# Statistics of one head group by way of DRAM, and four more chunks of products ahead of the first scores, in a two-layer encoder on one core

## The chip, the core and the metric

The kernel runs on one core of a Trainium2 chip. A core has a matrix engine (TensorE, in the profile PE for its matmuls and PEld for its weight loads), a vector engine (DVE), an activation engine (ACT), a general engine (GpSimd, POOL) and a queue for transfers (SyncE, SP); ACT and POOL can start transfers too. The metric is the device time of one launch in microseconds (us), as the median of the runs. The profile is that of one more execution, taken by the hardware profiler; its times are counted from the first instruction of its span.

## The reference

The input is x, 512 tokens of 1024 features, in float32. There are two layers; each is an attention and a SwiGLU feed-forward of width 2816, both with an RMS norm ahead and a residual behind, and a last RMS norm ends it. Layer 0 has 16 query heads on 4 key heads, a window of 128 tokens to either side, a penalty that grows with distance, and a learned sink logit for each head. Layer 1 is where most of the change lies:

```python
for gi, (win, dil) in enumerate(((128, 1), (512, 4), (2048, 16))):
    q, k, v = (to_residue(qkv[:, :, gi, n], dil) for n in range(3))
    o, lse = banded_attention(q, k, v, slopes, dil, win // (2 * dil), 64)
    outs.append(from_residue(o, b, dil)); lses.append(from_residue(lse, b, dil))
wts = softmax(stack(lses), axis=0)
o = einsum('gbsh,gbshd->bshd', wts, stack(outs))
x = x + o.reshape(b, s, 1024) @ w_out
```

For each of 16 head slots there are three groups of query, key and value. Group 0 attends to neighbours within 64 tokens; groups 1 and 2 to tokens of the same residue class modulo 4 and 16. The three outputs are added with weights from their softmax denominators. So whoever finishes a head slot needs, for each token, the maximum and the sum of the exponentials of group 0.

## The kernel before, in words

All activations lie transposed, features on the 128 partitions and the 512 tokens along the free dimension. Every product of float32 is made of three matmuls on operands that are split into a high and a low part (`mm3`, line 116). A weight unit is 128 output features by 1024 inputs: SP loads it into one of three buffers `wraw`, ACT writes the high part `wh` (line 92), DVE the low part `wl` (line 93). TensorE then runs it in 8 steps of 6 matmuls of 256 columns; such a step is a *chunk* here. Units of values (`values`, line 192, tile `psv`) have 16 chunks of the same 6 matmuls.

TensorE's instructions run in the order in which the program is written. The other engines' order is set by a scheduler when the program is built; each engine then runs its own list, and waits where a result of another engine is not there yet. The PSUM tiles go round in tags: three banks `mm`, two `sc`, two `tp`, one `ov`.

Since a chunk depends on nothing near it, chunks are used as filling. A generator `fill` hands them out, and `spread` and `weave` (lines 156 to 171) place a number of them between the steps of the attention: scores, turning of the probabilities (transposes on TensorE), weighing of the values.

**Layer 0, start.** The first key and query units end before the sum of squares is known. `norm_sums` (line 258) and `norm_rows` (line 267) then make 1/rms as columns and as rows; at the end of `norm_rows` the waiting keys and queries are scaled and split on DVE and ACT (lines 123 to 138, 310, 320). After it the program places 6 chunks of the unit of values, then the first scores, with chunks between them:

```python
spread([2, norm_sums, 4, norm_rows], early)
counts = [8, 9, 7, 6, 6, 6, 4, 4, 4, 4, 3, 2, 2, 2, 3, 3]
spread([6, s0, 1, s1, 1, s2, 1, s3, 2], fill)
```

`early` is that unit of values: 2 and 4 of its 16 chunks lie ahead of the rows, 10 behind them, then `fill` goes on with query units. Its four blocks of tokens are gathered in the banks `ov`, `sc`, `tp`, `mm`, 4 chunks each, and copied out by ACT (line 205, tile `v`). s0 to s3 are the scores of the first two attention units. Each has two score tiles, which take the two `sc` banks; DVE adds the distance table and takes the maximum (line 349), ACT takes the exponential with its sum (line 356), DVE the reciprocal (358), POOL multiplies (360), and TensorE turns the result (367). `counts` says how many chunks go into each of the 16 attention units that follow.

**Layer 1.** For each of 8 pairs of heads p, `attention_a(p)` does group 0 (four blocks t of 128 queries; `scores_a`, `turn_a`, `weigh_a`) and `attention_b(p)` groups 1 and 2 (`scores_b`, `turn_b`, `merge_rows`, `weigh_b`), each woven with 32 chunks (48 in the first). `scores_a` leaves in the tile `sta`, for each query on its partition, the negative maxima and the sums of two heads (lines 670 and 672). Group 0 has its queries in another order than groups 1 and 2, which work by residue class, so the statistics must change their order. `merge_turn` (line 783) turns `sta` on TensorE into 4 rows (tile `stt`), which DVE copies in the new order into `strow` (line 791); `merge_back` (line 798) turns these back with 4 small transposes (tile `stc`), and DVE copies them into `sa` (line 804). `scores_b` reads `sa` for the first time in its line 734, on DVE. So that the transpose sees 128 columns, `sta` is a padded tile that POOL sets to zero at the layer's start (line 590).

**End.** `final` (line 454) writes the last 256 tokens: transposes, a scaling by 1/rms on ACT and DVE, four transfers out.

## Time and profile before

| | us |
|---|---|
| median of 3 runs (range) | 1468.41 (1467.15 to 1469.77) |
| the profiled execution | 1470.46 |
| its span | 1468.3 |
| PE busy in the span | 1452.2 |
| DVE, ACT, POOL busy | 731.5, 613.4, 107.4 |
| mean granted TensorE clock | 0.995 of full |

The stages in the span: layer 0's attention with its projections until about 185, its feed-forward until 551, layer 1's attention until about 1098, its feed-forward until 1462, then the transfers out.

How to read it: a row of the timeline has start, duration, engine, line, operation, output<-inputs, count of merged instructions, and in brackets how long the engine had been idle and who released it. A row of the windows has, for a stretch of the span, its length, the busy time of TensorE (with the number of instructions), the granted clock, the share of the transfer engines and GB/s. Matmuls overlap in the pipeline, so that the time of one row is longer than the distance to the next; what a matmul costs is read from the distance of the starts.

### The profile page before, as it was taken

To read this page: it belongs to the slowest core of one execution; us is meant where nothing else is said; L and a number is where in the kernel's file an instruction comes from. 1 tells how busy PE (TensorE), PEld (TensorE's weight loads), DVE (VectorE), ACT (ScalarE), POOL (GpSimd) and SP (SyncE) were. 2 spreads that over 40 slices of the span, in tenths; PEclk is the share of its full clock that TensorE was granted. 3 is DMA by queue.
4 is the path that set the end of the run, shared out by engine and by line. 5 is a ranking of instruction groups with operands and counts; after the bars stand their busy time and mean duration, and the time that the engine had idled before them with its cause. 6 is when DMAs were issued, how large, how long until landed. Compare 5 with 4: busy or idle time off the path is not lost.

```text
span 1468.3 us, 29636 instructions
## 1 busy us (share of the span) xinstructions
PE 1452.2 (99%) x12834; PEld 1426.0 (97%) x12834; DVE 731.5 (50%) x1393; ACT 613.4 (42%) x1130; POOL 107.4 (7%) x150
## 2 busy tenths in 40 slices
PE   8999999999999999999999999999999999999998
PEld 8888999999999999999999999999999999999998
DVE  6677544444443335346556556556464444443223
ACT  5676442332223325435536536536343233222222
POOL 4234200000000100000000000000030000000111
PEclk9999999999999999999999999999999999999999
DMA  6110223223223232322122222221133223322231
GB/s 202 58 44 30 79 94 102 88 100 101 99 84 107 90 100 85 102 73 87 59 87 73 73 87 73 73 83 63 58 103 99 99 89 101 101 96 96 94 98 65
DMA packets 38354, 128.29 MB, mean 87 GB/s; under 512 B 4560, under 2 KB 6096, under 8 KB 38224
## 3 DMA queue, kind: packets, MB, share of 16 engines
q1 hardware_dynamic: 37792, 125.86, 25.8%
q8 instruction: 100, 1.64, 0.5%
q10 hardware_dynamic: 432, 0.54, 0.1%
q14 instruction: 30, 0.25, 0.1%
HBM read 124.29 MB, written 2.10 MB: 86 GB/s over the span
## 4 chain that ended last, share of the span: by engine, by line
PE 94%; ACT 2%; DVE 2%; issue 1%; DMA 0%; POOL 0%; SPq 0%; DVEq 0%; ACTq 0%; POOLq 0%
PE mm L121 51%; PE sc L121 16%; PE psv L121 10%; PE tp L121 8%; PE sc L718 1%; PE sc L659 1%; PE sc L143 1%; PE ov L381 1%; PE ov L773 1%; PE tp L367 1%; PE tp L681 1%; PE ov L700 1%; ACT pr L356 0%; PE tp L760 0%; DVE wl L93 0%
## 5 line engine op out<-in xcount | busy, mean ns | idle before, releaser
L92 ACT ACTIVATE wh<-wraw 128x1024 fp32r<-128x1024 f32 (+3 forms) x242 | 247.2, 1024 | 599.5 <-PE mm L121 254.4
L93 DVE TENSOR_TENSOR wl<-wraw,wh 128x1024 fp32r<-128x1024 f32 (+3 forms) x242 | 289.3, 1196 | 201.5 <-ACT wh L92 197.6
L121 PE MATMUL mm<-xh,wh 128*128 128x256 f32 x1632 | 331.5, 285 | 1.4 <-ACT wh L92 1.4
L121 PE MATMUL mm<-xh,wl 128*128 128x256 f32 x1632 | 321.4, 279 | 0.8 <-DVE wl L93 0.7
L121 PE MATMUL mm<-xl,wh 128*128 128x256 f32 x1632 | 321.4, 279 | 0.0
L121 PEld LDWEIGHTS mm<-xh,wh 128*128 128x128 f32 x1632 | 248.8, 189 | 7.2 <-issue 4.8
L121 PEld LDWEIGHTS mm<-xh,wl 128*128 128x128 f32 x1632 | 248.1, 189 | 1.3 <-DVE wl L93 1.2
L121 PEld LDWEIGHTS mm<-xl,wh 128*128 128x128 f32 x1632 | 248.8, 189 | 0.0
L235 POOL TENSOR_TENSOR ssum<-ssum,tmp 128x512 f32<-128x512 f32 x34 | 53.8, 1584 | 988.8 <-ACT tmp L231 974.1
L121 PE MATMUL psv<-wh,xh 128*128 128x256 f32 x288 | 83.2, 289 | 0.0
L121 PE MATMUL psv<-wl,xh 128*128 128x256 f32 x288 | 80.8, 281 | 0.0
L121 PE MATMUL psv<-wh,xl 128*128 128x256 f32 x288 | 80.8, 280 | 0.0
L121 PE MATMUL mm<-ah,wl 128*128 128x256 f32 x374 | 74.8, 276 | 0.0
L121 PE MATMUL mm<-ah,wh 128*128 128x256 f32 x374 | 74.8, 277 | 0.0
L121 PE MATMUL mm<-al,wh 128*128 128x256 f32 x374 | 74.6, 276 | 0.0
L121 PE MATMUL tp<-xh,wh 128*128 128x256 f32 x352 | 68.9, 277 | 0.0
L121 PE MATMUL sc<-xh,wh 128*128 128x256 f32 x352 | 68.8, 277 | 0.0
L121 PE MATMUL tp<-xh,wl 128*128 128x256 f32 x352 | 68.7, 276 | 0.0
L121 PE MATMUL tp<-xl,wh 128*128 128x256 f32 x352 | 68.6, 276 | 0.0
L121 PE MATMUL sc<-xh,wl 128*128 128x256 f32 x352 | 68.5, 276 | 0.0
L121 PE MATMUL sc<-xl,wh 128*128 128x256 f32 x352 | 68.5, 276 | 0.0
L121 PE MATMUL sc<-ah,wl 128*128 128x256 f32 x330 | 66.1, 276 | 0.0
(181 smaller groups left out, 2732.2 us busy)
## 6 DMA issues: line engine op xcount, KB each, us to landing
wraw<-wunits SPq DMA_DIRECT2D x191, 512.0 KB, 3.3
wraw<-wv SPq DMA_DIRECT2D x25, 512.0 KB, 3.4
wraw<-wunits SPq DMA_DIRECT2D x16, 384.0 KB, 2.9
x<-xT SPq DMA_DIRECT2D x8, 256.0 KB, 4.8
wraw<-wunits SPq DMA_DIRECT2D x4, 256.0 KB, 4.8
outT<-x SPq DMA_DIRECT2D x2, 384.0 KB, 2.8
wraw<-wunits SPq DMA_DIRECT2D x4, 128.0 KB, 4.8
tab<-tabs SPq DMA_DIRECT2D x1, 512.0 KB, 4.9
```

What stands on the lines that cost most here:

```text
L92: nc.scalar.activation(out_h, src, AF.Copy)
L93: nc.vector.tensor_tensor(out_l, src, out_h.bitcast(F32), op=OP.subtract)
L121: nc.tensor.matmul(out[:, cols], a, b[:, cols], start=first and k == 0 and c == 0, stop=last and k == 2, skip_group_check=True)
L143: nc.tensor.matmul(outs[a], qp[a][:, qc], k[a][:, kc], start=first and k is kp, stop=k is low, skip_group_check=True)
L235: nc.gpsimd.tensor_tensor(norm["sum"], norm["sum"], sq, op=OP.add)
L367: nc.tensor.transpose(tp[:, 256 * hf + 128 * i:256 * hf + 128 * i + 128], st["pr"][:, 2 * i + hf, 128 * kb:128 * kb + 128], ident)
L381: nc.tensor.matmul(ov[64 * hf:64 * hf + 64, :256], v0[:, k0 // 128 + kb, vs], st["pt", kb][:, 256 * hf:256 * hf + 256], start=(kb == 0), s ...
L659: nc.tensor.matmul(out, qk["qs", p][a][:, 128 * t:128 * t + 128], kp[k], start=t == ts[0] and k == 0, stop=k == 1, skip_group_check=True)
L681: nc.tensor.transpose(tp[:, (nb * a + kb) * 128:(nb * a + kb) * 128 + 128], st["pr", p, ts][:, a, o + 128 * kb:o + 128 * kb + 128], ident)
L700: nc.tensor.matmul(ov[rows, 128 * t - 64:128 * t + 64], v[:, t - 1 + kb, vs], pt[:, 256 * a + 128 * kb:256 * a + 128 * kb + 128], start=Fa ...
L718: nc.tensor.matmul(ps[a][:, o:o + 128], qk["q", p, 1 + g][rows, cols], qk["k", p, 1 + g][rows, cols], start=(o == 0), stop=True, skip_grou ...
L773: nc.tensor.matmul(ov[rows, 128 * c:128 * c + 128], vals[p // 2, 1 + g][:, c, hv + 64 * a:hv + 64 * a + 64], pts[g][:, 256 * a + 128 * (c ...
```

## The change

Three edits:

1. Layer 0: 10 chunks, not 6, lie between `norm_rows` and s0; the first four attention units get one chunk less each, so that the total is the same.
2. Layer 1: `merge_turn` and `merge_back` go. `merge` writes `sta` (now 16 numbers on each partition, without padding and without the zeroing) to a DRAM tile with two transfers and reads it back in the order of groups 1 and 2 with four, all started by POOL. In `attention_a` it stands ahead of the first turning; the turnings of t = 0 and 1 move one place back, and the number of places stays 13.
3. `final`: the tiles for the output are halves of two `wraw` buffers, and `last` takes a buffer of `tmp`.

```diff
-        counts = [8, 9, 7, 6, 6, 6, 4, 4, 4, 4, 3, 2, 2, 2, 3, 3]
+        counts = [7, 8, 6, 5, 6, 6, 4, 4, 4, 4, 3, 2, 2, 2, 3, 3]
...
-        spread([6, s0, 1, s1, 1, s2, 1, s3, 2], fill)
+        spread([10, s0, 1, s1, 1, s2, 1, s3, 2], fill)
...
-        last = spool.tile([128, 256], F32, name="last", bufs=1)
+        last = spool.tile([128, S], F32, name="tmp")[:, :256]
...
+        outs = [wpool.tile([128, D], F32, name="wraw") for _ in range(2)]
...
-                out = spool.tile([128, 512], F32, name="tmp" if k else "out")
+                out = outs[b][:, 512 * k:512 * k + 512]
...
-        stats = [pool.tile([128, 4, 32], F32, name=f"sta{k}", bufs=1) for k in range(2)]
-        for t in stats:
-            nc.gpsimd.memset(t, 0.0)
+        dram = ctx.enter_context(tc.tile_pool(name="dram", bufs=2, space=bass.MemoryType.DRAM))
...
-                st["sta", p] = stats[p % 2]
+                st["sta", p] = pool.tile([128, 4, 4], F32, name="sta")
...
-        def merge_turn(p):
-            ps = bank("tp", "stt")
-            nc.tensor.transpose(ps[:, :128], st["sta", p].rearrange("p t e -> p (t e)"), ident)
...
-        def merge_back(p):
...
+        def merge(p):
+            sta = st["sta", p]
+            by_query = dram.tile([S + 64, 4], F32, name="stats")
+            nc.gpsimd.dma_start(by_query[:S].rearrange("(t q) e -> q t e", t=4), sta)
+            nc.gpsimd.dma_start(by_query[S:], sta[:64, 0, :])
 
             sa = st["sa", p] = pool.tile([128, 4, 4], F32, name="sa")
-            nc.vector.tensor_copy(sa.rearrange("p c e -> p (c e)"), ps[:, :16])
+            by_class = by_query[64:].rearrange("(m c i) e -> i m c e", c=4, i=4)
+            for i in range(4):
+                nc.gpsimd.dma_start(sa[32 * i:32 * i + 32], by_class[i])
...
-                    lambda: turn((0, 1), 0), lambda: turn((0, 1), 1), lambda: merge_turn(p),
-                    lambda: turn((2, 3), 2), 0, lambda: turn((2, 3), 3), lambda: merge_back(p), 0, weigh]
+                    lambda: merge(p), lambda: turn((0, 1), 0), lambda: turn((0, 1), 1),
+                    lambda: turn((2, 3), 2), 0, lambda: turn((2, 3), 3), 0, 0, weigh]
```

How it moves instructions. First ACT's list in layer 0, from the last queries of the first scores (`qt`) to the exponentials of s0 to s3 (257 columns for s0 and s1, 385 for s2 and s3); `v` are the copies of the blocks of values, `wh` the high part of a weight unit:

```order
 L130 ACTIVATE qt_432<-tmp 64x512
 L130 ACTIVATE qt_433<-tmp 64x512
-L205 ACTIVATE v_99<-psv,rstd 128x256 x2
+L205 ACTIVATE v_99<-psv,rstd 128x256 x3
+L92 ACTIVATE wh<-wraw 128x1024
 L356 ACT_TABLE_LOAD
 L356 ACTIVATE pr,mst<-pr,mst 128x257 x4
+L92 ACTIVATE wh<-wraw 128x1024
 L356 ACTIVATE pr,mst<-pr,mst 128x385 x4
```

A third copy of values and two weight splits, which stood behind the exponentials, now stand ahead of them or among them.

Then DVE's list in layer 1, pair 0, from the turnings of group 0 to the stretch ahead of the first maxima of groups 1 and 2. Before:

```order
L93 TENSOR_TENSOR wl<-wraw,wh 128x1024
L791 COPY strow<-stt 4x4x16 x2
L791 COPY strow<-stt 4x8x16 x3
L615 TENSOR_TENSOR k_7191<-mm,rb 128x512
L93 TENSOR_TENSOR wl<-wraw,wh 128x1024
L633 COPY pt_7245<-tp 128x512
L804 COPY sa<-stc 128x16
L93 TENSOR_TENSOR wl<-wraw,wh 128x1024 x2
```

With the change (line 631 is the former 633, 613 the former 615):

```order
L93 TENSOR_TENSOR wl<-wraw,wh 128x1024
L631 COPY pt_7145<-tp 128x512
L613 TENSOR_TENSOR k_7190<-mm,rb 128x512
L93 TENSOR_TENSOR wl<-wraw,wh 128x1024
L631 COPY pt_7244<-tp 128x512
L93 TENSOR_TENSOR wl<-wraw,wh 128x1024 x2
```

The five copies to `strow` and the copy to `sa` are gone; a turning's copy (`pt`) moved behind a weight split.

Last, POOL's list with the change, from the end of layer 0 to the end of pair 0's statistics (788 and 787 write to DRAM, 793 reads back):

```order
L235 TENSOR_TENSOR ssum<-ssum,tmp 128x512 x14
L848 COPY acca<-ssum 128x512
L788 DMA stats<-sta 64x4
L787 DMA stats<-sta 128x4x4
L793 DMA sa<-stats 32x4x4 x4
```

The three rows of transfers stand there eight times, once for each pair; POOL has nothing else between them.

## The prediction

> **What bounds the kernel now.** I read the page's first part, then the chain of waits, then the timeline of the two places that the change touches.

> ```profile
> PE 1452.2 (99%) x12834; PEld 1426.0 (97%) x12834; DVE 731.5 (50%) x1393; ACT 613.4 (42%) x1130; POOL 107.4 (7%) x150
> ```

> TensorE is busy 99% of the span; nothing else comes near. So time falls only where TensorE gets less work, waits less, or runs at a higher clock. Its timeline around the first scores of layer 0, then ACT's, DVE's and POOL's:

> ```profile
> 36.15 0.28 PE L121 MATMUL psv<-wh,xl 128*128 128x256 f32 x1
> 38.68 0.39 PE L143 MATMUL sc<-kt,qt 128*128 128x256 f32 x1 [2.25 <-DVE qt L131]
> 38.90 0.28 PE L143 MATMUL sc<-kl,qt 128*128 128x256 f32 x1
> 40.41 0.58 PE L143 MATMUL sc<-kt,qt 128*128 128x256 f32 x1 [1.23 <-ACT v L205]
> ...
> 37.28 2.58 ACT L130 ACTIVATE qt<-tmp 64x512 fp32r<-64x512 f32 x4
> 39.89 0.84 ACT L205 ACTIVATE v<-psv,rstd 128x256 f32<-128x256 f32 x2
> 43.54 1.28 ACT L356 ACT_TABLE_LOAD   x1 [2.81 <-DVE mst L353]
> 44.83 0.51 ACT L356 ACTIVATE pr<-pr,mst 128x257 f32<-128x257 f32 x1
> ...
> 37.94 2.84 DVE L131 TENSOR_TENSOR qt<-tmp,qt 64x512 fp32r<-64x512 f32 x4 [1.43 <-ACT qt L130]
> 40.81 0.42 DVE L349 CUSTOM_DVE_ANT_0 pr<-sc,tab 128x256 f32<-128x256 f32 x1
> ...
> 48.07 4.10 POOL L360 TENSOR_SCALAR pr<-pr,mst 128x256 f32<-128x256 f32 x8 [24.88 <-DVE mst L358]
> ```

> TensorE runs out of chunks at 36.4 and waits twice: 2.25 us for the split queries, 1.23 us for a bank that ACT has to copy out. What follows is dearer than the waits themselves. The windows of TensorE, cut where the clock changes:

> ```profile
> 5.55:8.96 3.41, 1.96 (x14) 1.00 1.03 374
> 36.27:39.68 3.41, 0.66 (x4) 1.00 0.00 0
> 39.68:43.09 3.41, 2.68 (x12) 0.50 0.01 2
> 43.09:46.50 3.41, 3.41 (x16) 0.50 0.01 2
> 1056.84:1060.25 3.41, 2.42 (x19) 1.00 0.00 0
> ```

> The clock changes on a grid of 3.41 us. After a stretch with 0.66 us of work it is half for 6.8 us; a stretch with 1.96 us of work was followed by half clock too (8.96 to 12.37), one with 2.42 us was not. The price of a chunk stands in the chain of waits:

> ```profile
> 41.21 1.28 PE psv L121 x6
> ...
> 50.30 1.42 PE mm L121 x12
> ```

> 6 matmuls take 1.28 us at half clock, 0.71 us (0.118 each) at full.

> **The change part by part.** *Edit 1, ten chunks.* Ten chunks from the end of the rows' transposes at 31.95 last until 39.05; before, six lasted until 36.4. DVE splits a query tile in 0.71 us (2.84/4), so the first is ready at 38.65: the wait of 2.25 us is gone. The bank is not ready sooner, since ACT's rows ahead of its copy are unchanged: the second score still starts at 40.41, and a wait of about 1.0 us stays (39.45 to 40.41).

> From there I walk on with these rows: a read of scores on DVE 0.42 us, or 0.56 for 384 columns; table load 1.28; exponential 0.5; POOL 0.51 (4.10/8).

> ```profile
> 45.30 0.56 DVE L349 CUSTOM_DVE_ANT_0 pr<-sc,tab 128x384 f32<-128x384 f32 x1 [1.29 <-PE sc L143]
> ...
> L92 ACT ACTIVATE wh<-wraw 128x1024 fp32r<-128x1024 f32 (+3 forms) x242 | 247.2, 1024 | 599.5 <-PE mm L121 254.4
> L93 DVE TENSOR_TENSOR wl<-wraw,wh 128x1024 fp32r<-128x1024 f32 (+3 forms) x242 | 289.3, 1196 | 201.5 <-ACT wh L92 197.6
> ...
> 50.06 0.48 PE L121 MATMUL mm<-xh,wh 128*128 128x256 f32 x2
> ...
> 57.60 0.60 PE L367 MATMUL tp<-ident,pr 128*128 128x128 f32 x4
> ```

> TensorE: s0 ends 40.65, a chunk to 41.35, s1 to 41.97 (0.14 us for a bank), a chunk to 42.67, s2 to 43.35, a chunk to 44.05. s3 needs the banks of s2. DVE has read s1 by 42.72, splits the weights that now stand there (to 43.95), reads s2's first tile by 44.66; its next instruction waits for s0's exponentials. ACT makes them after three copies (41.15), a weight split (42.2) and the table load (43.5), so by 44.6; DVE reads s2's second tile by 45.42. s3 thus waits 0.67 and 0.42 us and ends at 45.82; two chunks to 47.2. The first turning needs POOL's four heads, which I place at 47.27, and ends at about 47.7. Before, the first chunk after that turning starts at 50.06. So TensorE is 2.4 us earlier there, and four chunks further (2.8 us): **5.2 us**. It loses 2.2 us in new or remaining waits, nowhere more than about 1.0 us in any stretch of 3.41, which leaves about 2.4 us of work, as much as in the stretch at 1056.84 that kept full clock. Bounds: 7.4 us if those waits vanish, 1.8 us if half clock comes back for two stretches (3.4 us).

> [...]

> The first four attention units give the four chunks back, one each (0.7 us). What covers that is the lead of the softmax: POOL finishes the second unit's four heads at 52.17 (48.07 and 4.10) and TensorE turns them at 57.60, 5.4 us later. If that cover were short, each unit would cost up to 0.7 us, 2.8 in all. I take 0.

> *Edit 2, the statistics.* TensorE loses, for each pair, one transpose and four small ones:

> ```profile
> 630.69 0.39 PE L121 MATMUL mm<-xh,wl 128*128 128x256 f32 x2
> 630.92 0.27 PE L786 MATMUL stt<-ident,sta 128*128 128x128 f32 x1
> 630.95 0.48 PE L121 MATMUL mm<-xh,wh 128*128 128x256 f32 x2
> 631.26 0.40 PE L121 MATMUL mm<-xl,wh 128*128 128x256 f32 x2
> ...
> 641.59 0.28 PE L121 MATMUL psv<-wh,xl 128*128 128x256 f32 x1
> 641.79 0.41 PE L801 MATMUL stc<-ident,strow 4*128 4x4 f32 x4
> 642.13 0.39 PE L121 MATMUL psv<-wh,xh 128*128 128x256 f32 x1
> 642.35 0.28 PE L121 MATMUL psv<-wl,xh 128*128 128x256 f32 x1
> ...
> 572.00:1056.00 484.00, 484.00 (x4488) 473.95 (x4487) 261.91 (x665) 241.64 (x549) 0.00 (x0) 1.00 0.23 77
> ```

> From 630.69 to 631.26 pass 0.57 us in which four matmuls of 0.118 run: the transpose costs 0.10. From 641.59 to 642.35 pass 0.76 us for two matmuls: the four small ones cost 0.52, dear for their size. So 0.62 us a pair, **5.0 us** for eight. In this stage TensorE is busy 484.00 of 484.00 us, so this comes off the end. DVE's six copies lie beside TensorE's work and give nothing.

> What is added lies on POOL and the transfer queues. POOL is free there (0.00 us busy). The new wait: DVE's line 734 reads `sa`, and everything behind it on DVE waits with it. From the last sum of group 0 to that line pass, in the last pair, 22.4 us:

> ```profile
> 1027.85 0.19 ACT L672 ACTIVATION_READ_ACCUMULATOR pr<-pr,sta 128x1 f32 x1
> ...
> 1050.43 0.16 DVE L734 SCALAR_TENSOR_TENSOR mb<-mb,sa 128x4 f32<-128x4 f32 x1
> ...
> 827.99 1.70 ACT L750 ACTIVATE pr<-pr,mb 128x256 f32<-128x256 f32 x4
> ...
> 833.74 0.60 PE L760 MATMUL tp<-ident,pr 128*128 128x128 f32 x4
> ...
> g_sb<-gains ACTq DMA_DIRECT2D x1, 20.0 KB, 3.0
> qs_sb<-qsc SPq DMA_DIRECT2D x1, 8.0 KB, 4.8
> L235 POOL TENSOR_TENSOR ssum<-ssum,tmp 128x512 f32<-128x512 f32 x34 | 53.8, 1584 | 988.8 <-ACT tmp L231 974.1
> ```

> No row shows a transfer started by POOL. Nearest: small transfers land after 3.0 to 4.8 us, and POOL's longest kind of row takes 1.58. One way out and one back is 6.0 us at least; six starts at 1.58 and two landings of 4.8 are 19.1. Both ends are under 22.4: the way is hidden, cost 0.

> *Edit 3 and the zeroing* change tiles at the end and POOL work that nobody waits for; the waits in the engines' lists at the end are the same. Cost 0; its bounds are a few tenths either way.

> **Sum.** 1470.46 − 5.2 − 5.0 = 1460.3 for an execution like the profiled one. The median lies 2.05 us lower; if that execution had less half clock at the first scores, edit 1 gives it less, at worst 1.7 (half a stretch of 3.41) less. 1468.41 − 10.2 = 1458.2 and 1459.9: I take **1459.0**.

> **Rivals.** *A: the softmax takes over.* s3 and the first turning wait longer than I walked, work in a stretch falls towards 1.96 us and half clock returns. For it: my stretch sits right at 2.4; three waits follow each other. Against: it needs another 0.4 us. It costs 1.7 to 3.4 us: 1460.7 to 1462.4.

> *B: slower, POOL's starts are held up.* If POOL can start transfers only while DVE is idle (DVE is busy 261.91 of 484, so 46% is left), the six starts take 9.5/0.46 = 20.6 and the way 30 us. TensorE turns group 1 and 2's result 4.05 us after it is ready (833.74 against 829.69), so pairs 0 to 6 lose 3.8 us and the last 7.8: +34 − 10, about 1493. Break-even is where 7·(T−26.4)+(T−22.4) = 10.2, a way of 27 us. Against it: the six starts would have to be as dear as POOL's longest rows. [...]

> *C: the way is between 22.4 and 27 us*, so that part of edit 2 is given back: about 1463.

> *D: edit 1 alone fails to move anything* because ACT, not the queries, was the limit (the second wait hangs on ACT already): 1463.

> **How the numbers follow.** Forecast 0.63, A 0.19, B 0.07, C 0.06, D 0.05. The forecast's own range is 1457 to 1460.7 (the waits may shrink, the two baselines differ); with A, C and D up to 1464, and to 1456 for waits that vanish in part. Within 0.2% (about 2.9 us, what a measurement here can tell) I leave 0.04, from B near its break-even and D with C together; slower 0.07; faster 0.89.

> **What would show it.** Right: the first scores released by ACT alone, clock 1.00 from 32 to 60 us, the first turning near 47.7, no `stt` or `stc`, TensorE busy 100% between 572 and 1056 with that stage 5 us shorter, line 734's counterpart waiting for DVE's own reads only. Wrong: half clock after 39 us (A), DVE idle in front of the line that reads `sa` with a transfer as releaser (B, C), or TensorE waiting for splits in the first four units.

## The result, and the profile after

The changed kernel takes **1459.96 us** (median of 4 runs, 1459.58 to 1460.20), the kernel before beside it 1467.78 us (4 runs, 1466.91 to 1469.77): ratio 0.9945, 95% interval 0.9927 to 0.9962. In a later comparison five runs gave 1459.93 us against 1468.98 us: 0.9941, 0.9927 to 0.9954. Forecast were 1459.0 us, range 1456 to 1464, a gain of 9.4 us; the two comparisons show 7.8 and 9.05. The total came out; two of its terms did not, in opposite directions.

The first part of the page, then TensorE's timeline of the changed kernel, from the transposes of the rows to the first turning:

```profile
PE 1444.4 (99%) x12794; PEld 1418.7 (97%) x12794; DVE 717.7 (49%) x1345; ACT 612.4 (42%) x1130; POOL 135.7 (9%) x196
```

```profile
31.45 0.60 PE L272 MATMUL rrow<-ident,rstd 128*128 128x128 f32 x4
...
38.83 0.28 PE L121 MATMUL psv<-wh,xl 128*128 128x256 f32 x1
38.95 0.28 PE L143 MATMUL sc<-kt,qt 128*128 128x256 f32 x1
...
40.29 0.39 PE L143 MATMUL sc<-kt,qt 128*128 128x256 f32 x1 [0.94 <-ACT v L205]
...
44.27 0.45 PE L143 MATMUL sc<-kt,qt 128*128 128x384 f32 x1 [0.17 <-DVE mst L349]
...
45.04 0.44 PE L143 MATMUL sc<-kt,qt 128*128 128x384 f32 x1 [0.15 <-DVE mst L349]
...
46.89 0.60 PE L367 MATMUL tp<-ident,pr 128*128 128x128 f32 x4
47.24 0.48 PE L121 MATMUL mm<-xh,wh 128*128 128x256 f32 x2
```

The wait for the split queries is gone (the score at 38.95 has no bracket), the wait for ACT's bank stays at 0.94 us, s3 waits 0.17 and 0.15 us. The windows of TensorE between the clock's steps:

```profile
38.97:42.38 3.41, 2.47 (x21) 1.00 0.01 2
42.38:45.79 3.41, 3.09 (x20) 1.00 0.33 96
```

Full clock all the way. Before, the same work ran 6.8 us at half clock.

Now three landmarks that both kernels have. The transposes of the rows start at 31.59 before and 31.45 after (0.14 us from the loading ahead of them). The sums of squares at the start of layer 1, first before, then after:

```profile
556.33 0.94 PE L239 MATMUL ssq<-ones,ssum 128*128 128x1 f32 x8
```

```profile
551.96 0.95 PE L239 MATMUL ssq<-ones,ssum 128*128 128x1 f32 x8
```

4.37 us earlier, less the 0.14: **edit 1 is worth 4.2 us** in this pair of traces (forecast 5.2). The last pair's first turning of groups 1 and 2, before and after:

```profile
1058.98 0.33 PE L760 MATMUL tp<-ident,pr 128*128 128x128 f32 x1 [0.52 <-ACT pr L750]
```

```profile
1049.08 0.33 PE L759 MATMUL tp<-ident,pr 128*128 128x128 f32 x1 [0.52 <-ACT pr L749]
```

9.90 us earlier, so **edit 2 is worth 5.5 us** (forecast 5.0). It grows by 0.64 to 0.75 us from pair to pair. From there on the distance stays 9.9 us to the last transposes of the result (1461.71 and 1451.81), and the spans differ by 9.9 (1468.3 and 1458.4): **edit 3 gives and costs nothing**.

**Where edit 1 lost a microsecond.** At the first turning TensorE is 2.82 us earlier (50.06 to 47.24) with four chunks more behind it, 5.5 us in all by 0.118 us a matmul and less the 0.14; at the landmark in layer 1 only 4.2 are left. One place takes most of it: the second score block of the first unit. TensorE's timeline before, where the scores come without a wait:

```profile
58.50 0.39 PE L121 MATMUL mm<-xh,wl 128*128 128x256 f32 x2
58.73 0.28 PE L143 MATMUL sc<-kt,qt 128*128 128x256 f32 x1
...
59.20 0.40 PE L121 MATMUL mm<-xh,wh 128*128 128x256 f32 x2
```

After:

```profile
54.99 0.39 PE L121 MATMUL mm<-xh,wl 128*128 128x256 f32 x2
55.89 0.39 PE L143 MATMUL sc<-kt,qt 128*128 128x256 f32 x1 [0.51 <-DVE mst L349]
56.11 0.28 PE L143 MATMUL sc<-kl,qt 128*128 128x256 f32 x1
56.37 0.39 PE L143 MATMUL sc<-kt,qt 128*128 128x256 f32 x1
56.59 0.28 PE L143 MATMUL sc<-kl,qt 128*128 128x256 f32 x1
56.71 0.39 PE L121 MATMUL mm<-xh,wh 128*128 128x256 f32 x2
```

From the start of the chunk's last row to the next chunk pass 0.70 us before, 1.72 us after: 1.0 us, of which the bracket shows only 0.51. The first score starts 0.90 us behind that row in place of 0.23, which is 0.67 us; the bracket is shorter, since it counts from the row's modelled end (54.99 and 0.39). Then the starts lie 0.22, 0.26 and 0.22 us apart in place of 0.12. The 0.26 is a second wait for DVE, for the other bank, and shows only in TensorE's loads of weights:

```profile
56.37 0.19 PEld L143 LDWEIGHTS sc<-kt,qt 128*128 128x128 f32 x1 [0.18 <-DVE mst L349]
```

So the 1.0 us are 0.67 and 0.14 of waiting and twice 0.10, because the matmul behind each of the two late ones starts 0.22 us after it and not 0.12. DVE is what both wait for:

```profile
53.56 1.68 DVE L131 TENSOR_TENSOR qt<-tmp,qt 64x512 fp32r<-64x512 f32 x2
55.27 0.56 DVE L349 CUSTOM_DVE_ANT_0 pr<-sc,tab 128x384 f32<-128x384 f32 x1
```

The splits of a query unit that has just been finished stand ahead of the reads of the last scores, which free the banks. With other counts of chunks the unit ends at another place among the scores.

**The way through DRAM**, in the last pair: POOL's timeline, the reads' group, and DVE's timeline where the numbers are used.

```profile
1019.13 0.78 POOL L787 DMA_DIRECT2D stats<-sta  x1 [3.85 <-ACT pr L671]
1022.05 2.19 POOL L793 DMA_DIRECT2D sa<-stats  x4 [2.14 <-DMA stats<-sta]
```

```profile
L793 POOL DMA_DIRECT2D sa<-stats x32: 552/552/561, 622.6 to 1023.7; - x32
...
DMA to landing us min/median/max: 1.8/2.8/4.6
```

```profile
1040.42 0.08 DVE L730 DVE_READ_ACCUMULATOR2_ANT mb<- 128x1 f32 x1
1040.53 0.16 DVE L733 SCALAR_TENSOR_TENSOR mb<-mb,sa 128x4 f32<-128x4 f32 x1
```

From the start of the write to the landing of the last read pass 7.2 to 8.7 us over the eight pairs; from the write to line 733 pass 21.4 (31 in pair 0). No bracket stands at 1040.53: DVE goes on from its own reads. One of the 32 reads, the last of pair 6, started late:

```profile
968.74 0.56 POOL L793 DMA_DIRECT2D sa<-stats  x1 [0.61 <-issue]
```

DVE was not what held it: its last instruction, a copy, had ended at 967.95 us, 0.18 us before POOL fell idle.

### The profile page after: what moved, and what is told of

Read it like the earlier page. It is cut to its first block, busy times and chain, and to the rows that moved or that the text cites. A ratio compares the mean times of both kernels' runs of the same rounds, so it can differ in the third digit from the quotient of the medians.

```text
span 1458.4 us, 29596 instructions
## 1 busy us (share of the span) xinstructions
PE 1444.4 (99%) x12794; PEld 1418.7 (97%) x12794; DVE 717.7 (49%) x1345; ACT 612.4 (42%) x1130; POOL 135.7 (9%) x196
## 4 chain that ended last, share of the span: by engine, by line
PE 95%; ACT 2%; DVE 1%; issue 0%; DMA 0%; POOL 0%; SPq 0%; DVEq 0%; ACTq 0%; POOLq 0%
PE mm L121 52%; PE sc L121 16%; PE psv L121 9%; PE tp L121 8%; PE ov L381 1%; PE sc L717 1%; PE sc L658 1%; PE ov L772 1%; PE sc L143 1%; PE tp L367 1%; PE tp L680 1%; PE ov L699 1%; PE tp L759 0%; DVE wl L93 0%; DMA x<-xT 0%
## 5 line engine op out<-in xcount | busy, mean ns | idle before, releaser
L92 ACT ACTIVATE wh<-wraw 128x1024 fp32r<-128x1024 f32 (+3 forms) x242 | 247.4, 1024 | 591.3 <-PE mm L121 241.4
L93 DVE TENSOR_TENSOR wl<-wraw,wh 128x1024 fp32r<-128x1024 f32 (+3 forms) x242 | 290.4, 1201 | 205.2 <-ACT wh L92 200.4
L121 PE MATMUL mm<-xh,wh 128*128 128x256 f32 x1632 | 329.4, 283 | 1.1 <-ACT wh L92 1.1
L121 PE MATMUL mm<-xh,wl 128*128 128x256 f32 x1632 | 321.6, 279 | 1.0 <-DVE wl L93 0.9
L121 PE MATMUL mm<-xl,wh 128*128 128x256 f32 x1632 | 321.2, 278 | 0.0
L121 PEld LDWEIGHTS mm<-xh,wh 128*128 128x128 f32 x1632 | 248.6, 189 | 7.0 <-issue 4.8
L121 PEld LDWEIGHTS mm<-xh,wl 128*128 128x128 f32 x1632 | 248.2, 189 | 1.4 <-DVE wl L93 1.4
L121 PEld LDWEIGHTS mm<-xl,wh 128*128 128x128 f32 x1632 | 248.5, 189 | 0.2 <-DVE xl L221 0.2
L235 POOL TENSOR_TENSOR ssum<-ssum,tmp 128x512 f32<-128x512 f32 x34 | 53.1, 1562 | 523.9 <-ACT tmp L231 471.3
L121 PE MATMUL psv<-wh,xh 128*128 128x256 f32 x288 | 82.4, 286 | 0.0
L121 PE MATMUL psv<-wl,xh 128*128 128x256 f32 x288 | 80.2, 278 | 0.0
L121 PE MATMUL psv<-wh,xl 128*128 128x256 f32 x288 | 80.1, 278 | 0.0
L121 PE MATMUL mm<-ah,wh 128*128 128x256 f32 x374 | 74.8, 277 | 0.0
L121 PE MATMUL mm<-ah,wl 128*128 128x256 f32 x374 | 74.7, 276 | 0.0
L121 PE MATMUL mm<-al,wh 128*128 128x256 f32 x374 | 74.7, 276 | 0.0
L121 PE MATMUL tp<-xh,wh 128*128 128x256 f32 x352 | 68.8, 277 | 0.0
L121 PE MATMUL sc<-xh,wh 128*128 128x256 f32 x352 | 68.7, 277 | 0.0
L121 PE MATMUL tp<-xh,wl 128*128 128x256 f32 x352 | 68.7, 276 | 0.0
L121 PE MATMUL tp<-xl,wh 128*128 128x256 f32 x352 | 68.7, 276 | 0.0
L121 PE MATMUL sc<-xh,wl 128*128 128x256 f32 x352 | 68.5, 276 | 0.0
L121 PE MATMUL sc<-xl,wh 128*128 128x256 f32 x352 | 68.5, 276 | 0.0
L121 PE MATMUL sc<-ah,wl 128*128 128x256 f32 x330 | 66.0, 276 | 0.0
```

The source lines that it names most:

```text
L92: nc.scalar.activation(out_h, src, AF.Copy)
L93: nc.vector.tensor_tensor(out_l, src, out_h.bitcast(F32), op=OP.subtract)
L121: nc.tensor.matmul(out[:, cols], a, b[:, cols], start=first and k == 0 and c == 0, stop=last and k == 2, skip_group_check=True)
L235: nc.gpsimd.tensor_tensor(norm["sum"], norm["sum"], sq, op=OP.add)
```

## The experiments

**Edit 1 alone**, on the kernel before:

```diff
-        counts = [8, 9, 7, 6, 6, 6, 4, ...
+        counts = [7, 8, 6, 5, 6, 6, 4, ...
-        spread([6, s0, 1, s1, 1, s2, 1, s3, 2], fill)
+        spread([10, s0, 1, s1, 1, s2, 1, s3, 2], fill)
```

> Edit 1 alone. Theory (the waits ahead of the first scores bring half clock, and ten chunks remove both): granted clock 1.00 from 32 to 60 us, one wait of about 0.9 us for ACT's bank, and the kernel before less 2 to 5 us, by how many half-clock stretches its executions had; the runs lie within 1 us of each other, where those of before spread over 3 us. With 5.5 us for edit 2 as the two traces show it, the median would be about 1465.3. Rival D (ACT was the limit, nothing moves): within 1 us of before. Rival (the half clock has another cause): half clock still there after 39 us, 2 us gained, spread as before.

1466.01 us (11 runs, 1464.45 to 1467.18) against 1468.90: ratio 0.9978, 0.9970 to 0.9987. The clock is full from 32 to 60 us and the wait for the bank 0.94 us. Its sums of squares start 4.3 us earlier than before's, counted from the same landmark: edit 1's price is the same in the second trace. The medians give it less, 2.9 us (more on that in the part on the baseline, below). D is out. The spread did not shrink to 1 us as expected; it is 2.7 us, and two other things that differ between executions show in the traces below.

**Edits 2 and 3 without edit 1**, that is the changed kernel with the old counts:

```diff
-        counts = [7, 8, 6, 5, 6, 6, 4, ...
+        counts = [8, 9, 7, 6, 6, 6, 4, ...
-        spread([10, s0, 1, s1, 1, s2, 1, s3, 2], fill)
+        spread([6, s0, 1, s1, 1, s2, 1, s3, 2], fill)
```

> Edits 2 and 3 without edit 1 (six chunks and the old counts). Theory (TensorE loses 0.62 to 0.68 us per pair, nothing waits for the way through DRAM, edit 3 is nothing): before less 5.0 to 5.5 us, 1462.3 to 1462.8; TensorE's wait of 2.3 us and half clock at the first scores are still there, and the runs spread by about 3 us as before's do. Rival (edit 3 or the way costs something): above 1463.5, with a wait at the end or ahead of the line that reads sa.

1461.95 us (1461.50 to 1464.20) against 1468.90: 0.9960, 0.9948 to 0.9973, 7.0 us in the medians, more than the 5.0 to 5.5 expected. In the trace the part from the scores of pair 0 to the end of the attention gains 5.2 us. The wait of 2.25 us and the half clock at the first scores are back:

```profile
35.26:38.67 3.41, 1.16 (x10) 1.00 0.00 0
38.67:42.09 3.42, 2.21 (x11) 0.50 0.01 2
...
554.09:557.50 3.41, 3.16 (x30) 1.00 0.27 106
575.00:600.00 25.00, 25.00 (x215) 1.00 0.27 85
```

The last two rows are where traces differ for reasons that no edit touches. After the one-column matmuls of the sums of squares half clock followed in the traces before and after (554.38 to 557.79 in the latter), and not here; it costs 1.6 us. And in the 25 us from 575 on TensorE starts 215 matmuls here and 223 in the trace after, both at full clock and never idle:

```profile
575.00:600.00 25.00, 25.00 (x223) 1.00 0.36 115
```

Single starts are 118 ns apart in the one and 113 in the other, for the whole stretch from about 563 to 605 us: 1.6 us again. So the sum of the two medians (2.9 and 7.0) says less than the stages of the traces.

**Eight chunks**, the first two units with one more each:

```diff
-        counts = [7, 8, 6, 5, 6, 6, 4, ...
+        counts = [8, 9, 6, 5, 6, 6, 4, ...
-        spread([10, s0, 1, s1, 1, s2, 1, s3, 2], fill)
+        spread([8, s0, 1, s1, 1, s2, 1, s3, 2], fill)
```

> The changed kernel with 8 chunks in place of 10 ahead of the first scores; the first two units get one more each. Theory (a stretch of 3.41 us with under about 2.2 us of work brings half clock): TensorE idles 1.0 us before the first score and 1.5 before the second, some 0.9 to 2.1 us of work in a stretch by where the grid falls; at full clock about +0.9 us over the changed kernel, with half clock +2.6 to +4.3; so the runs lie between 1460.9 and 1464.3 and spread by more than 1.5 us. Rival (waits alone count): +0.9 us, 1460.9, all runs within 0.7 us, clock 1.00.

1461.46 us, five runs at 1458.95, 1459.32, 1461.46, 1462.87 and 1463.23. Two lie under the theory's range, and the spread does not speak for it: the changed kernel spreads by 3.4 us too (1459.10 to 1462.49, below). The one traced kept full clock, the rival's sign, and its sums of squares in layer 1 start 0.6 us later than the changed kernel's, counted from the same landmark, near the 0.9 us of the waits alone. It kept full clock at

```profile
36.47:39.88 3.41, 1.88 (x15) 1.00 0.00 0
39.88:43.29 3.41, 2.66 (x21) 1.00 0.01 2
```

1.88 us of work in a stretch were enough here. The prediction drew the line between 1.96 and 2.42; that line was wrong. By these windows (1.16 dropped, 1.88 kept) it lies lower. Whether one of the other four runs had half clock there is not shown.

**One chunk of the units moved**: 8, 8, 6, 5, 5 for 7, 8, 6, 5, 6.

```diff
-        counts = [7, 8, 6, 5, 6, 6, 4, ...
+        counts = [8, 8, 6, 5, 5, 6, 4, ...
```

> The changed kernel with 8, 8, 6, 5, 5 chunks in the first five units in place of 7, 8, 6, 5, 6. Theory (the wait of 0.51 us at 55.4 us, a score that waits for a bank that DVE reads late, is there because the first unit gave up a chunk): that wait is gone and the time is 0.5 us less, 1459.4. Rival (DVE's queue is the limit whatever TensorE has to do): the wait moves to another unit, and the time stays within 0.2 us of 1460.0.

1459.94 us (1458.59 to 1461.11), no difference that can be told. The wait at 55.4 is gone, and one like it stands in a later unit, again behind two splits of queries on DVE:

```profile
95.70 0.38 PE L143 MATMUL sc<-kt,qt 128*128 128x256 f32 x1 [0.57 <-DVE mst L349]
```

That is the rival's picture: the collision moves with the chunks. By the trace the units lose 1.0 us here, 1.3 in the changed kernel.

**The changed kernel again**, beside the next three.

> The changed kernel itself, beside the others of this call. The trace of the changed kernel against that of before gives 4.2 us for edit 1 and 5.5 for edit 2, 9.7 in all; edit 1 alone gave 2.9 in the medians and edits 2 and 3 alone 7.0, 9.9 in all. If the edits add up, it runs 9 to 10 us under the kernel before; the first comparison showed 7.8. Rival (the edits share a gain): 7 to 8 us.

1459.93 us against 1468.98: 9.05 us. Its runs fall into two groups, 1459.1 to 1459.9 and 1462.4 to 1462.5; the traced one is 1462.49 and has the rhythm of 118 ns after 560 us, which makes it 1.6 us later at the scores of pair 0 than the first trace of the same kernel. The gains add up within that.

**Eleven chunks**:

```diff
-        counts = [7, 8, 6, 5, 6, 6, 4, ...
+        counts = [8, 8, 6, 5, 5, 5, 4, ...
-        spread([10, s0, 1, s1, 1, s2, 1, s3, 2], fill)
+        spread([11, s0, 1, s1, 1, s2, 1, s3, 2], fill)
```

> Eleven chunks ahead of the first scores, units of 8, 8, 6, 5, 5, 5 chunks. Theory (ACT's bank copy alone holds the second score, and DVE, which reads both heads after its splits of queries, holds the softmax): the wait ahead of the second score falls from 0.94 to about 0.2 us, DVE's first read of scores starts when it did, and the time is 0.3 to 0.7 us under the changed kernel. Rival (every chunk more ahead of the scores is taken back by waits in the units): within 0.2 us of it, with new waits of scores for DVE between 50 and 130 us.

1460.42 us (1457.73 to 1461.23), ratio to before 0.9939, 0.9926 to 0.9951: not to be told from the changed kernel. The traced run is the fastest of the five. It shows both sides:

```profile
40.20 0.39 PE L143 MATMUL sc<-kt,qt 128*128 128x256 f32 x1 [0.24 <-ACT v L205]
...
43.55 0.44 PE L143 MATMUL sc<-kt,qt 128*128 128x384 f32 x1 [0.94 <-DVE mst L349]
...
45.58 0.45 PE L143 MATMUL sc<-kt,qt 128*128 128x384 f32 x1 [0.34 <-DVE mst L349]
```

What the bank no longer costs (0.94 to 0.24) comes back at s2 and s3, which wait for DVE's reads. But no score waits in the units, and at the scores that start at 100.61 us before, TensorE is 5.3 us ahead, counted from the sums of squares at 27.87 us, where the changed kernel is 4.2. So 5.2 us were there to be had; in the changed kernel the collisions in the units took the difference.

**Four small transposes put back**, that wait for nobody and that nobody reads:

```diff
+        def small(p):
+            ps = bank("tp", "stc")
+            for c in range(4):
+                nc.tensor.transpose(ps[:, 4 * c:4 * c + 4], ident[:4, :], ident[:4, :4])
...
-                    lambda: turn((2, 3), 2), 0, lambda: turn((2, 3), 3), 0, 0, weigh]
+                    lambda: turn((2, 3), 2), 0, lambda: turn((2, 3), 3), lambda: small(p), 0, 0, weigh]
```

> The changed kernel with four transposes of 4 by 4 per pair put back, which read the identity matrix and wait for nobody, and whose result nobody reads. Theory (they are dear by themselves, 0.13 us each): 0.52 a pair, 4.2 us over the changed kernel. Rival (the 0.52 us were a wait for DVE's copies, and four such matmuls take about 0.03 each): 1 us over it.

1465.28 us, 5.4 over the changed kernel beside it. In the trace the distance grows by 4.3 us over seven pairs, 0.61 each. The timeline, and the loads of weights of these four:

```profile
635.84 0.28 PE L121 MATMUL psv<-wh,xl 128*128 128x256 f32 x1
636.05 0.40 PE L785 MATMUL stc<-ident 4*128 4x4 f32 x4
636.38 0.39 PE L121 MATMUL psv<-wh,xh 128*128 128x256 f32 x1
636.60 0.28 PE L121 MATMUL psv<-wl,xh 128*128 128x256 f32 x1
```

```profile
L785 PEld LDWEIGHTS stc<-ident x32: 133/136/138, 636.0 to 1033.7; 4*128 4x128 f32 x32
```

0.76 us for two matmuls and the four, as before, with no DVE in it: they are dear by themselves, but not by 0.13 us each. In the trace the four start 0.06 to 0.08 us apart and take 0.33 us together, up to the next matmul's start (636.05 to 636.38). The rest lies at the two ends: the first of them starts 0.21 us after the matmul ahead of it (635.84), and the second matmul behind them 0.22 us after the first (636.38 to 636.60), in place of 0.11 to 0.12. Why the stream stumbles there is not shown. The load of weights is not the price: each load's row is 136 ns long for 4 rows of 128, but they overlap (before, the four that start at 641.79 take 0.32 us together), and the removed `stt`, whose 128x128 load took 143 ns, cost only 0.10 us.

**Four more ways** out and back between the gathered numbers and line 733, and **two more**:

```diff
+            for k in range(4):        # the other run: 2
+                way = dram.tile([128, 4, 4], F32, name="way")
+                nc.gpsimd.dma_start(way, sa)
+                sa = pool.tile([128, 4, 4], F32, name="sb")
+                nc.gpsimd.dma_start(sa, way)
+            st["sa", p] = sa
```

> The changed kernel with four more ways out and back between the gathered statistics and the line that reads them. One way took 7.2 to 8.7 us in the trace, each further one should take 5.5 to 6, so the whole is 30 to 32 us against 21.4 us from the write to that line. Theory of the prediction (21.4 us for the last pair and about 4 more for the others are covered, all beyond is paid by TensorE, with half clock after each wait): 44 to 56 us of waits and 14 to 27 of half clock, 58 to 83 us over the changed kernel, DVE idle ahead of that line with a transfer as its releaser. Rival (more is covered than I think, since TensorE has other work ahead of it): under 20 us.

> The changed kernel with two more ways out and back, of about 5.2 us each by the run with four more (27 to 30 us in all there). Theory: the way becomes 17 to 19 us, under the 21.4 us from the write to the line that reads sa; DVE does not wait for a transfer there, and the time is the changed kernel's, within what half clock and the two rhythms do (1459 to 1462.5). Rival (it is not the way's end that counts but POOL's starts or what the transfers take from others): a third to a half of the loss of the run with four more, 10 to 17 us.

With four more: 1493.06 us (2 runs), ratio 1.0164, 1.0146 to 1.0183, 33 us over the changed kernel, between the theory's 58 and the rival's 20. The whole way takes 26.3 to 29.9 us, each further one 5.2. Pair 1, DVE's timeline, TensorE's, and the windows behind it:

```profile
714.79 0.16 DVE L733 SCALAR_TENSOR_TENSOR mb<-mb,sb 128x4 f32<-128x4 f32 x1 [4.75 <-DMA sb<-way]
```

```profile
719.42 0.33 PE L759 MATMUL tp<-ident,pr 128*128 128x128 f32 x1 [4.03 <-ACT pr L749]
```

```profile
716.69:720.10 3.41, 0.33 (x1) 1.00 0.00 0
720.10:723.51 3.41, 3.29 (x16) 0.50 0.00 0
...
1013.65:1017.06 3.41, 1.61 (x14) 1.00 0.00 0
1017.06:1020.48 3.42, 2.71 (x20) 1.00 0.00 0
```

The chain is the predicted one: transfer, line 733, ACT's exponentials, TensorE's turning, then half clock. Its size is smaller. TensorE's waits at these turnings are 18 us over the usual, where the prediction's rule with these ways gives 23 (six pairs above 25.4 us, the last above 21.4); the 44 to 56 us expected came of a way of 30 to 32 us. And half clock follows in five stretches, where I had counted on one or two per pair; TensorE has 13.7 us of work in them, so they cost 6.8 us. The second turning of each pair waits too (2.7 us over the usual in all). That makes 27.5 of the 33 us; the rest is not broken down here. After 1.61 us of work the clock stayed full.

With two more: 1461.09 us (two runs, 1461.81 and 1460.37). The way takes 16.9 to 21.6 us. In seven pairs DVE does not wait; in the last, where it is 21.6 us, the group of line 733 has

```profile
its engine sat idle before it (us, times) until:
  DMA sb<-way: 0.2, 1
```

So DVE's wait begins at the 21.4 us where the trace put it, and a way more than twice as long as the change's own is hidden: TensorE's wait at that turning is 0.56 us where the changed kernel has 0.52.

**A version with eleven chunks and, in layer 1, four chunks between the two groups of one-column matmuls**:

```diff
-        norm_sums(True)
-        run(k_first[1])
+        groups = token_blocks(range(4))
+        ps = bank("tp", "ssq")
+        add_up(ps, norm["sum"], groups, True, True)
+        spread([4], k_first[1])
+        add_up(ps, norm["by class"], [(4 + b, tok) for b, tok in groups], False, True)
+        norm_columns(ps, 0, 8)
+        run(k_first[1])
```

> Eleven chunks and units of 8, 8, 6, 5, 5, 5 as in the run before, and in layer 1 four chunks of the first key unit between the two groups of one-column matmuls that add up the squares (two groups of eight, one behind the other so far). Theory (at that place half clock came in 6 of 10 traces, where 14 to 16 of these matmuls fell into one stretch of 3.41 us; with four chunks between them a stretch holds eight to ten and keeps its clock): clock 1.00 from 32 us to the end of TensorE's work, the wait of 0.26 us there gone; together with about 1 us from eleven chunks 2 us under the changed kernel, about 1458, and the runs closer together, apart from the two rhythms of matmuls (113 and 118 ns) after 560 us, worth 1.6. Rival (those one-column matmuls are not what brings half clock): half clock at about 555 us still there, 1 us under the changed kernel at most.

1459.17 us (1459.08 to 1460.41) against 1469.02: 0.9933, 0.9919 to 0.9947. The traced run has full clock from 32 us on:

```profile
32.00:1450.00 1418.00, 1414.42 (x12579) 1.00 0.26 84
```

Its runs lie closer together than the changed kernel's. The gain over the changed kernel, 0.8 us in the medians of two comparisons, is not beyond what a measurement tells; the traced run has the 118 ns rhythm after 560 us, which takes 1.6 us of what full clock gave. One trace without half clock there proves little by itself (5 of 11 other traces have none either). What speaks for the cure is the count of columns in the part on half clock below: the two stretches with the sums of squares hold 5384 and 5640 columns here, well above the line. That the cure holds in every execution is not shown.

## Why the prediction was right

- **What bounds the kernel**: right. Both gains are TensorE's, one from waits and clock, one from work taken away.
- **Edit 1, the walk to the first turning**: right. 47.24 against 47.7 walked, 5.5 us against 5.2; the bank's wait 0.94 against 1.0; s3's two waits came, at 0.17 and 0.15 us for 0.67 and 0.42, since DVE had read s2's two tiles 0.4 to 0.5 us sooner than walked.
- **Edit 1, "the first four units give the four chunks back; I take 0"**: wrong, and the step that made edit 1 a microsecond too large. It looked at POOL's lead over the turnings. What ran short was DVE's: a query unit that ends three chunks into the first unit puts 1.68 us of splits ahead of the reads of scores, and TensorE waits for the banks that these reads free. 1.3 us, 1.0 of it in one place; with other counts it moves, with eleven chunks it is gone.
- **Half clock**: right that it goes with the waits (full clock in every trace with 8, 10 or 11 chunks, 6.8 us of half clock in both traces with six). The line was mis-sized, and busy time cannot draw it: stretches with 1.61 us of work (four more ways) and 1.88 (eight chunks) kept full clock, one with 1.16 (six chunks) did not; in the loading phase one with 1.93 us kept it (eight chunks, from 12.57), and one with 2.22 did not (the changed kernel, from 4.83), like the 1.96 that I leaned on.
- **What separates them** in all twelve traces is the number of columns of the matmuls that start in a stretch, 256 for one of a chunk and one for a one-column matmul. Of 5077 stretches at full clock, 15 hold 2832 columns or fewer, and half clock follows on 14 of them (the other, with 2688, lies among the first loads of the run of edits 2 and 3 alone). Of the five with 3072 to 3086 it follows on two, and of those with 3328 or more on none. From half clock the way back goes by the same line: three stretches with 3072 columns or fewer were followed by half clock again, sixteen with 3456 or more by full clock. This is a count over the traces; no run was made to test it. The emptiest stretch at the first scores holds 512 columns before and 4608 in the changed kernel, so rival A was further off than it got credit for; with eight chunks it holds 3072, so that its full clock was luck by this count. The half clock at the first scores came with gaps of 2.25 and 1.23 us (before) or 1.21 (edits 2 and 3 alone), each shorter than a stretch.
- **Edit 2, 0.10 + 0.52 a pair**: right in kind, a little small. The put-back of the four small ones cost 0.61 a pair, not the 0.52 between two neighbours; all eight pairs gave 5.2 to 5.5 us, not 5.0. Where the 0.09 between lie is not shown.
- **Edit 2, the way**: right. 7.2 to 8.7 us, inside 6.0 to 19.1, under 21.4. POOL's starts take 552 to 561 ns in all 32 reads, and the one that came late, by 0.61 us, came while DVE was idle: rival B's mechanism did not show. In the last pair the four reads take 2.19 us from 1022.05, 0.55 each, the first two while DVE works without a gap (1021.59 to 1023.50, a split and the copy `pt`). C would need a way more than twice as long.
- **The baseline**: the 2.05 us between the profiled execution and the median were put down to less half clock at the first scores. The traces neither show nor exclude it: both with six chunks have the full 6.8 us. The granted clocks of all runs speak for it. In the comparison with edit 1 alone their mean is 0.9965 in 15 runs before and 0.9983 in 11 with the edit, which makes about 5 us of half clock less (an estimate: twice the difference, times the span); in the comparison with eleven chunks and the small transposes the 15 runs before have 0.9974 and the 21 with edit 1 0.9980, about 2 us. So the executions before had on average less than the 6.8 us of the two traces, which fits that edit 1 gives the medians less than 4.2 us. Two more things vary: half clock after the sums of squares (6 of 12 traces, 1.6 us) and the rhythm after 560 us (118 ns in 7 of 12, another 1.6 us). That 1459.0 came within 1 us of 1459.96 is in part luck: edit 1 was 1.0 us too large and edit 2 0.5 too small.

## What to carry to other kernels

Where one engine is busy to 99%, look for waits on it that are dearer than their brackets: here 3.5 us of brackets brought 6.8 us of half clock, and a bracket of 0.51 us stood for 1.0, with a second wait in the loads of weights behind it. When filler is moved ahead of a stall, walk the places it is taken from for every engine that frees something there, not only for the one that was last. Four tiny matmuls in a dense stream cost more here than four of 256 columns (0.52 to 0.61 us against 0.47), and a round trip through DRAM on an idle queue was the cheaper transpose, since the first use is further off than the way: 21 us against 9.
